# Cross heads turned on TensorE instead of through transfers, and the residual on ScalarE and GpSimd, in a one-layer hybrid decoder step

## The chip, the cores and the metric

The kernel runs on one core of one Trainium2 chip. The metric is the device time of one execution in microseconds, as the median of several runs. PE is TensorE, DVE VectorE, ACT ScalarE, POOL GpSimd and SP SyncE, whose queue issues most DMA transfers here.

## What is computed

One inference step of a decoder layer, for 4096 new tokens of one sequence and for 8 x 8 tokens that continue cached sequences, all in float32 with a model width of 1024. The input is normalised and projected to 2816 columns. These feed three groups of heads: a gated short convolution (256 columns), sliding-window attention with window 128 (8 query heads, 2 key/value heads of width 64, one learned sink each), and cross attention with 4 heads into 256 memory tokens. The gated outputs, 1024 columns, go through an output projection, a normalisation, and are added to the input.

```python
h = _rmsnorm(x, g_pre)
z = h @ w_in
cb, cc, ch, cg, q, k, v, ag, mq, mg = _split_cols(z)
...
o_b = _window_prompt(q, k, v, sink_g)
out_b = jax.nn.silu(ag) * o_b
o_c = _mem_attend(mq.reshape(n, t, MEM_HEADS, HEAD_DIM), mem_k, mem_v)
out_c = jax.nn.silu(mg) * o_c
y = jnp.concatenate([out_a, out_b, out_c], axis=-1) @ w_out
return x + _rmsnorm(y, g_post), new_conv, new_k, new_v
```

## The kernel before

The program has two stages. The first, the input projection, runs the three phases of `input_projection` and stores queries, keys, values and gates in DRAM; in its third phase it also computes the memory's keys and values and the attention of groups 0 and 1, and begins group 2 (`third_jobs`, `first_chunk`). The second stage is the attention and output projection of 32 blocks of 128 rows. This text calls one pass of its loop a round.

A *group* is the attention of one 128-row block: its scores on PE (`bands` into `ws`, `crosses` into `xs`), two softmaxes, and the products with the values (`values`, into `pv`). The stage is pipelined over groups: in round i, `values_and_scores` emits the scores of group i+3 and the values of group i+1, while `Block.run` projects block i. A block's projection is two halves of 512 output columns, `y` with p = 0 and p = 1, each of 24 matmuls (8 slices, and 3 products of high and low parts). `events_of` says at which half and slice of the block the other work is emitted.

The value product needs the probabilities transposed, with keys on the partitions. For groups 0 and 1 PE transposes them (`band_transposes`, `cross_transposes`). From group 2 on, `moved` does it: a VectorE instruction transposes every 32x32 square in place, then SP issues 16 transfers inside SBUF, each of 32 partitions by 256 columns (32 KB), that bring the squares to their partitions. `turn_band` does so for the window heads (tile `sm`, result `wt`), `turn_cross` for the cross heads (tile `xp`, result `xt`): 32 transfers a round. `masks` then has GpSimd cut the window out of `wt` with four selects (copies in `wd`). The cross heads' probabilities are scaled by GpSimd (`cross_weights`) before they are turned.

A block ends in two parts that are kept for the next round's `scores` (`tails`): `scale` squares the second half on ScalarE and takes the reciprocal root (its power on GpSimd, tile `yst`), and `store` adds the scaled result `yn` to the input rows `xr` with one VectorE instruction and stores `xr`. There are two `xr` buffers and one `yn`. The load of a later block's `xr` waits on SP for the store from the same buffer.

A planner orders the instructions of each engine. VectorE's, from round 1 to 30, are held to the order in which the program emits them, as are the transposes of the squares, the masks, and the split of a block's input into `mh` and `ml`. In `tiled`, a run of attention matmuls is held to program order after its first; the output projection's matmuls are placed by the planner. `work` hands out tiles of 1024 columns from a pool of three.

In PSUM, `ws` has banks b0 to b3, `xs` b4 and b5, the first half of `y` shares b0, and `pv` has two banks of which the second half of `y` uses one. The few decode tokens are handled by `sample_mem` and `sample_window`, whose steps are spread over rounds 26 to 30; their loads (`sq`, `svm`, `skc`, `svc`) go through SP too.

Of the kernel before, what the change touches and what calls it, by code (L numbers as in the profile page):

```python
# [8 lines left out]
F32 = mybir.dt.float32  # L9
# [3 lines left out]
ALU = mybir.AluOpType  # L13
AX = mybir.AxisListType

P = 128
D = 1024
KT = D // P
# [33 lines left out]
def hybrid_layer(ctx: ExitStack, tc: tile.TileContext, a: dict):  # L52
# [1059 lines left out]
    class Group:  # L1112
# [3 lines left out]
            self.chunk, self.i, self.b = chunk, i, 2 * chunk.c + i  # L1116
            self.pt, self.pv, self.xpt, self.cross_sums = {}, {}, {}, {}

        def open_scores(self, n):
            b = self.b  # L1120
            if n == 0:
                t = wp.tile([P, D], F32, tag="sm", name=f"sm{b}", bufs=1) if b % 2 and b > 1 else work(f"sm{b}")
                self.sm = t.rearrange("p (h k j) -> p h k j" if b < 2 else "p (k h j) -> p h k j", h=8, k=4)
                self.flat_sm = t
            if n == 3:
                t = wp.tile([P, D], F32, tag="p", name=f"xp{b}", bufs=1) if b % 2 and b > 1 else work(f"xp{b}")
                self.p = t.rearrange("p (h a k j) -> p h a k j" if b < 2 else "p (k h a j) -> p h a k j", h=4, a=2, k=4)
                self.flat_p = t

        def early_scores(self, n):  # L1130
            self.open_scores(n)
# [12 lines left out]
        def scores(self):  # L1144
            self.open_scores(0)
            self.open_scores(3)
# [75 lines left out]
        def early_transposes(self, n):  # L1222
            if n == 0:
                pt = work(f"wpt{self.b}").rearrange("p (u n) -> p u n", u=2)
                pv = work(f"wpv{self.b}").rearrange("p (u n) -> p u n", u=2) if self.b else None
                for u in range(2):
                    self.pt[u], self.pv[u] = pt[:, u], pv[:, u] if self.b else None
            if n == 2:
                xpt = work(f"xpt{self.b}").rearrange("p (u n) -> p u n", u=2)
                for u in range(2):  # L1230
                    self.xpt[u] = xpt[:, u]
            if n < 2:
                self.band_transposes(n, psum(0, f"wt{self.b}_{n}"))
            else:
                self.cross_transposes(n - 2, psum(0, f"xt{self.b}_{n}"))

        def moved(self, squares, name):

            tc.keep_in_program_order(V.transpose(squares, squares))
            to = wp.tile([P, 4, 256], F32, tag=name, name=f"{name}{self.b}")  # L1240
            src = squares.rearrange("p (k n) -> p k n", k=4)
            for g in range(4):
                for k in range(4):
                    DMA.dma_start(to[32 * k : 32 * k + 32, g], src[32 * g : 32 * g + 32, k])
            return to

        def turn_band(self):
            self.w = self.moved(self.flat_sm, "wt").rearrange("p g (h i) -> p g h i", h=8)
# [26 lines left out]
        def cross_transposes(self, u, t):  # L1275
            t3 = t.rearrange("p (k n) -> p k n", k=2)
            for kt in range(2):
                for j in range(2):
                    TE.transpose(t3[:, kt, j * P : (j + 1) * P], self.p[:, 2 * u + j, kt].rearrange("p k j -> p (k j)"), ident)
            (S.copy if u else V.tensor_copy)(self.xpt[u], t)  # L1280

        def cross_values(self, o):
            c = self.chunk
            for j in range(2):
                x = (lambda hh, kt: self.xpt[hh][:, CT * kt + P * j : CT * kt + P * j + P]) if self.b < 2 else lambda hh, kt: self.x[:, :, 2 * hh + j, kt]
# [145 lines left out]
    def sample_window():  # L1431
# [22 lines left out]
        both = work("ssm")[:, : 4 * 192].rearrange("p (a n) -> p a n", a=4)  # L1454
# [30 lines left out]
        pt, ptn = work("swpt").rearrange("p (a n) -> p a n", a=2)[:, 0], work("swptn")[:64, :512]  # L1485
# [21 lines left out]
    class Block:  # L1507
# [28 lines left out]
        def run(self, last, events):  # L1536
# [6 lines left out]
            for p, (c0, c1) in enumerate(parts):  # L1543
# [6 lines left out]
                for k in range(KT):  # L1550
                    for fn in events.get((min(p, 1), k), ()) if p < 2 else ():
                        fn()
                    for l, r in ((0, 0), (1, 0), (0, 1)) if m == P else ((0, 0), (0, 1)):
                        TE.matmul(acc, self.hl[l][:, k], wo[k][c0 // 512][:, r, c0 % 512 : c0 % 512 + c1 - c0], start=j == 0, stop=j == passes * KT - 1)  # L1554
                        j += 1
                if m < P:
                    S.copy(yn[:m, c0:c1], acc[m : 2 * m])
# [19 lines left out]
                    V.tensor_tensor(yn[:m, 768:D], acc[:m], gpost[:m, 768:D], op=ALU.mult)  # L1577

            def store():
                for cs in (slice(0, 512), slice(512, D)) if last else (slice(0, D),):  # L1580
                    V.scalar_tensor_tensor(self.xr[:m, cs], yn[:m, cs], st[:m, 3:4], self.xr[:m, cs], op0=ALU.mult, op1=ALU.add)  # L1581
                    DMA.dma_start(dst[:, cs], self.xr[:m, cs])
# [23 lines left out]
    def events_of(i):  # L1606

        ev = {}

        def at(p, k, fn, *args):  # L1610
            ev.setdefault((p, k), []).append(lambda: fn(*args))

        at(0, 0 if i else 3, values_and_scores, i)
        if i + 2 < len(blocks):
            at(0, 0, blocks[i + 2].load)
        if i % 2 == 0:
            at(0, 1 if i else 4, chunk_load, i // 2 + 3)
# [135 lines left out]
```

## Time and profile before

| | |
|---|---|
| median of 3 runs | 1812.81 us (1812.52 to 1813.56) |
| the profiled execution | 1814.48 us, span 1812.8 us |
| PE busy | 1537.6 us (85%) |
| weight loads | 1380.1 us (76%) |
| VectorE busy | 1197.3 us (66%) |
| ScalarE busy | 732.0 us (40%) |
| GpSimd busy | 344.2 us (19%) |
| mean granted PE clock | 0.926 |
| SP's queue | 262.47 MB in 194501 packets |
| transfers inside SBUF | 480 `wt<-sm`, 480 `xt<-xp`, 32 KB each |

The profile is one execution. Rows of a group give the line, the engine, the operation, output and inputs by the program's names, the shapes and the count, then the busy time, the mean duration of one, and the idle time of the engine just before with what ended it. Line 62 stands for all VectorE instructions of rounds 1 to 30, and line 1044 for all attention matmuls, so these groups are told apart by their tiles. Rows of a timeline give start, length and a merged run of like instructions. Rows of stretches give start and end, the length, the busy times, the granted PE clock as a share of full speed, the share of the 16 DMA engines' time that was busy, and GB/s.

### The profile page before, as it was taken

To read this page: it belongs to the slowest core of one execution; us is meant where nothing else is said; L and a number is where in the kernel's file an instruction comes from. 1 tells how busy PE (TensorE), PEld (TensorE's weight loads), DVE (VectorE), ACT (ScalarE), POOL (GpSimd) and SP (SyncE) were. 2 spreads that over 40 slices of the span, in tenths; PEclk is the share of its full clock that TensorE was granted. 3 is DMA by queue.
4 is the path that set the end of the run, shared out by engine and by line. 5 is a ranking of instruction groups with operands and counts; after the bars stand their busy time and mean duration, and the time that the engine had idled before them with its cause. 6 is when DMAs were issued, how large, how long until landed. Compare 5 with 4: busy or idle time off the path is not lost. (4 is left out here: it accounts for less than half of the span.)

```text
span 1812.8 us, 31491 instructions
## 1 busy us (share of the span) xinstructions
PE 1537.6 (85%) x11471; PEld 1380.1 (76%) x11471; DVE 1197.3 (66%) x1920; ACT 732.0 (40%) x1844; POOL 344.2 (19%) x522
## 2 busy tenths in 40 slices
PE   9999999999999999999995776678667766777548
PEld 9999999999999999999994555456555555555336
DVE  7788888998877797677684654455546545654414
ACT  6766565642222244454362333333333333333212
POOL 0223332230000000001002322233123223322200
PEclk9999999999999999999997898888888888988679
DMA  9989998776432379677877455543554554343342
GB/s 259 215 230 268 269 237 297 245 211 233 165 107 107 121 258 306 222 238 231 247 286 204 131 158 156 154 113 121 150 156 133 155 156 138 111 136 116 121 157 82
DMA packets 236175, 335.29 MB, mean 185 GB/s; under 512 B 62453, under 2 KB 164853, under 8 KB 235989
## 3 DMA queue, kind: packets, MB, share of 16 engines
q1 hardware_dynamic: 194501, 262.47, 46.9%
q0 software_dynamic: 40800, 69.76, 14.8%
q8 instruction: 91, 1.49, 0.4%
q10 hardware_dynamic: 720, 1.05, 0.2%
q14 instruction: 63, 0.52, 0.1%
HBM read 192.54 MB, written 110.15 MB: 167 GB/s over the span
## 5 line engine op out<-in xcount | busy, mean ns | idle before, releaser
L1554 PE MATMUL y<-wo,mh 128*128 128x512 f32 (+1 forms) x1040 | 340.2, 400 | 41.3 <-DVE sm L62 13.1
L1554 PEld LDWEIGHTS y<-wo,mh 128*128 128x128 f32 x1040 | 198.4, 192 | 103.1 <-issue 33.5
L377 DVE TENSOR_TENSOR z<-c,z 128x520 f32<-128x520 f32 (+1 forms) x308 | 195.0, 646 | 88.8 <-PE c L370 88.0
L1554 PE MATMUL y<-wo,ml 128*128 128x512 f32 (+1 forms) x520 | 204.8, 394 | 0.0
L1044 PE MATMUL pv<-xt,mv 128*64 128x128 f32 x480 | 54.4, 398 | 176.6 <-DMA xt<-xp 108.8
L1044 PEld LDWEIGHTS pv<-xt,mv 128*64 128x64 f32 x480 | 43.9, 207 | 188.2 <-issue 181.8
L1212 ACT ACTIVATE xp<-xs,xnm 128x256 f32<-128x256 f32 x128 | 58.9, 473 | 260.8 <-issue 127.7
L1220 POOL TENSOR_SCALAR xp<-xp,xrd 128x256 f32<-128x256 f32 x128 | 62.4, 502 | 490.5 <-DVE xrd L62 404.0
L1195 ACT ACTIVATE sm<-sm,wnm 128x128 f32<-128x128 f32 x256 | 99.1, 389 | 116.9 <-DVE wnm L62 113.8
L62 DVE TENSOR_TENSOR mix<-mix,pv 128x256 f32<-128x256 f32 (+1 forms) x32 | 16.3, 551 | 159.0 <-PE pv L1044 153.8
L1554 PEld LDWEIGHTS y<-wo,ml 128*128 128x128 f32 x520 | 100.2, 193 | 20.5 <-issue 2.0
L62 DVE TENSOR_TENSOR place<-place,pv 128x256 f32<-128x256 f32 (+1 forms) x28 | 14.3, 551 | 134.3 <-PE pv L1044 134.3
L1178 ACT COPY sm<-ws 128x256 f32<-128x256 f32 x128 | 41.2, 376 | 68.1 <-PE ws L1044 43.2
L1562 ACT ACTIVATE y<-y 128x512 f32<-128x512 f32 (+1 forms) x66 | 38.4, 582 | 72.4 <-DVE yn L62 63.8
L1258 POOL TENSOR_SCALAR_AFFINE_SELECT wd<-wt 128x512 f32<-128x512 f32 (+1 forms) x60 | 60.8, 1013 | 32.0 <-DMA wt<-sm 16.5
L1044 PEld LDWEIGHTS ws<-kst,q 64*128 64x128 f32 x768 | 48.9, 190 | 11.6 <-issue 5.6
L62 DVE SCALAR_TENSOR_TENSOR xr<-yn,yst,xr 128x1024 f32<-128x1024 f32 x30 | 42.8, 1427 | 21.1 <-POOL yst L1575 21.0
L1044 PE MATMUL ws<-kst,q 64*128 64x256 f32 x768 | 56.5, 293 | 0.0
L1044 PE MATMUL pv<-wt,vh 128*64 128x256 f32 x240 | 53.0, 583 | 0.0
L745 POOL MEMSET negs<- 128x1 f32 x1 | 0.1, 98 | 264.4 <-PE c L370 264.4
L283 ACT ACTIVATE nat<-nat 104x1024 f32<-104x1024 f32 x40 | 42.2, 1056 | 15.7 <-DMA nat<-in_x_p 15.7
L1195 ACT ACTIVATION_READ_ACCUMULATOR sm<-sm,wnm 128x1 f32 x256 | 48.1, 188 | 0.0
(979 smaller groups left out, 4971.0 us busy)
## 6 DMA issues: line engine op xcount, KB each, us to landing
q<-qd POOLq DMA_DIRECT2D x32, 768.0 KB, 9.1
xr<-in_x_p SPq DMA_DIRECT2D x32, 512.0 KB
nat<-in_x_p SPq DMA_DIRECT2D x39, 416.0 KB
o_yp<-xr SPq DMA_DIRECT2D x31, 512.0 KB
wt<-sm SPq DMA_DIRECT2D x480, 32.0 KB
xt<-xp SPq DMA_DIRECT2D x480, 32.0 KB
md<-th POOLq DMA_DIRECT2D x48, 260.0 KB, 7.4
qd<-zh SPq DMA_DIRECT2D x48, 260.0 KB
```

The lines of the kernel that those rows point to most:

```text
L62: return (lambda *args, **kw: tc.keep_in_program_order(fn(*args, **kw))) if self.on else fn
L283: S.activation(t[:RG], t[:RG], AF.Square, accum_out=r[:RG, i : i + 1])
L377: add = lambda dst, other: V.tensor_tensor(dst, c, other, op=ALU.add)
L745: G.memset(third["negs"], NEG)
L1044: ins = TE.matmul(o, w, x, **kw)
L1178: S.copy(to, squares(s3[:, :, P : 2 * P]))
L1195: S.activation(sm[:, h], sm[:, h], AF.Exp, bias=nm[:, h : h + 1], scale=SCALE, accum_out=den[:, h : h + 1])
L1212: S.activation(p[:, i], s[:, i].rearrange("p (a k j) -> p a k j", a=2, k=4), AF.Exp, bias=nm[:, i : i + 1], scale=SCALE, accum_out=den[:, ...
L1220: G.tensor_scalar(p[:, i], p[:, i], rd[:, i : i + 1], 0.5, op0=ALU.mult, op1=ALU.mult)
L1258: G.affine_select(out, src, pattern=[[32 * sign, 2], [0, 8], [sign, 32]], compare_op=op, fill=0.0, base=base * sign, channel_multiplier=-s ...
L1554: TE.matmul(acc, self.hl[l][:, k], wo[k][c0 // 512][:, r, c0 % 512 : c0 % 512 + c1 - c0], start=j == 0, stop=j == passes * KT - 1)
L1562: square = lambda acc=acc, p=p, c0=c0, c1=c1, end=end: S.activation((psum(2, "sq") if end else acc)[:m, : c1 - c0], acc[:m], AF.Square, sc ...
```

## The change

The cross heads of all groups are now transposed on PE. `turn_cross` calls `cross_transposes` twice, on banks b1 and b2, which makes eight 128x128 transposes and two ScalarE copies into tiles `xpt`. `moved` is gone; `turn_band` keeps its in-place square transpose and its 16 transfers. The transposes come at the start of the block's second half for group i+2, and the masks of group i+2 right behind them instead of in the first half; the first slice of each half, and each slice at which something is emitted, starts with a matmul that is held in program order.

`store` scales `yn` on ScalarE and adds it to `xr` on GpSimd, in place of the one VectorE instruction (but for the last block and the decode block).

The pool `work` has one 1024-column tile instead of three, and one tile of 2048 columns, `pair`; a group's window and cross probabilities lie in one 2048-column tile, in `pair` for even groups (and for groups 0 and 1) and in a tile of `wp` for odd ones. The decode window's tiles are cut from `pair` too.

```diff
-        third["work"] = right.enter_context(tc.tile_pool(name="work", bufs=3, side="right"))
+        third["work"] = right.enter_context(tc.tile_pool(name="work", bufs=1, side="right"))
...
+    def pair(name):
+        return third["work"].tile([P, 2 * D], F32, tag="uu", name=name)
+
+    def in_order_here(ins):
+        if ps is not None:
+            tc.keep_in_program_order(ins)
...
-        def open_scores(self, n):
+        def open_scores(self):
             b = self.b
+            t = wp.tile([P, 2 * D], F32, tag="s", name=f"s{b}", bufs=1) if b % 2 and b > 1 else pair(f"s{b}")
+            self.flat_sm, self.flat_p = t[:, :D], t[:, D:]
...
-        def moved(self, squares, name):
-            tc.keep_in_program_order(V.transpose(squares, squares))
-            to = wp.tile([P, 4, 256], F32, tag=name, name=f"{name}{self.b}")
-            src = squares.rearrange("p (k n) -> p k n", k=4)
+        def turn_band(self):
+            tc.keep_in_program_order(V.transpose(self.flat_sm, self.flat_sm))
+            to = wp.tile([P, 4, 256], F32, tag="w", name=f"w{self.b}")
+            squares = self.flat_sm.rearrange("p (k n) -> p k n", k=4)
             for g in range(4):
                 for k in range(4):
-                    DMA.dma_start(to[32 * k : 32 * k + 32, g], src[32 * g : 32 * g + 32, k])
-            return to
+                    DMA.dma_start(to[32 * k : 32 * k + 32, g], squares[32 * g : 32 * g + 32, k])
+            self.w = to.rearrange("p g (h i) -> p g h i", h=8)
...
         def turn_cross(self):
-            self.x = self.moved(self.flat_p, "xt").rearrange("p g (h a i) -> p g h a i", h=4, a=2)
+            for u in range(2):
+                self.xpt[u] = wp.tile([P, 512], F32, tag="xpt", name=f"xpt{self.b}_{u}")
+                self.cross_transposes(u, psum(1 + u, f"xt{self.b}_{u}"))
...
-                    TE.transpose(t3[:, kt, j * P : (j + 1) * P], self.p[:, 2 * u + j, kt].rearrange("p k j -> p (k j)"), ident)
-            (S.copy if u else V.tensor_copy)(self.xpt[u], t)
+                    in_order_here(TE.transpose(t3[:, kt, j * P : (j + 1) * P], self.p[:, 2 * u + j, kt].rearrange("p k j -> p (k j)"), ident))
+            S.copy(self.xpt[u], t)
...
+                    ordered = b > 0 and (j == 0 or p < 2 and (min(p, 1), k) in events)
...
+                        if ordered:
+                            tc.keep_in_program_order(ins)
+                        ordered = False
...
             def store():
+                if not last and b != 32:
+                    tc.keep_in_program_order(S.mul(yn, yn, st[:, 3:4]))
+                    G.tensor_tensor(self.xr, yn, self.xr, op=ALU.add)
+                    DMA.dma_start(dst, self.xr)
+                    return
...
-        if i == 0:
-            at(0, 4, turn, 1, 2)
-        at(0, 4, turn, 2, i + 2)
+        at(1, 0 if i else 2, turn, 1, i + 2)
+        at(1, 1, turn, 2, i + 2)
...
         at(1, 2, turn, 0, i + 3)
-        at(1, 2, turn, 1, i + 3)
```

More of the change, by code (lines that the diff above doesn't have):

```diff
@@ L1117, in __init__, with early_scores @@
             self.pt, self.pv, self.xpt, self.cross_sums = {}, {}, {}, {}
-        def open_scores(self, n):
+        def open_scores(self):
             b = self.b
-            if n == 0:
[L1122 to L1131, printed above, removed]
+            t = wp.tile([P, 2 * D], F32, tag="s", name=f"s{b}", bufs=1) if b % 2 and b > 1 else pair(f"s{b}")
+            self.flat_sm, self.flat_p = t[:, :D], t[:, D:]
+            self.sm = self.flat_sm.rearrange("p (h k j) -> p h k j" if b < 2 else "p (k h j) -> p h k j", h=8, k=4)
+            self.p = self.flat_p.rearrange("p (h a k j) -> p h a k j", h=4, a=2, k=4)
+        def early_scores(self, n):
+            if n == 0:
+                self.open_scores()
             if n < 2:
@@ L1144, in scores @@
         def scores(self):
-            self.open_scores(0)
-            self.open_scores(3)
+            self.open_scores()
             bands = [psum(n, f"ws{self.b}_{n}").rearrange("p (h k) -> p h k", h=2) for n in range(4)]
@@ L1224, in early_transposes @@
                 pt = work(f"wpt{self.b}").rearrange("p (u n) -> p u n", u=2)
-                pv = work(f"wpv{self.b}").rearrange("p (u n) -> p u n", u=2) if self.b else None
+                pv = self.flat_sm.rearrange("p (u n) -> p u n", u=2) if self.b else None
                 for u in range(2):
@@ L1235, in early_transposes @@
                 self.cross_transposes(n - 2, psum(0, f"xt{self.b}_{n}"))
-        def moved(self, squares, name):
-            tc.keep_in_program_order(V.transpose(squares, squares))
-            to = wp.tile([P, 4, 256], F32, tag=name, name=f"{name}{self.b}")
-            src = squares.rearrange("p (k n) -> p k n", k=4)
+        def turn_band(self):
+            tc.keep_in_program_order(V.transpose(self.flat_sm, self.flat_sm))
+            to = wp.tile([P, 4, 256], F32, tag="w", name=f"w{self.b}")
+            squares = self.flat_sm.rearrange("p (k n) -> p k n", k=4)
             for g in range(4):
                 for k in range(4):
-                    DMA.dma_start(to[32 * k : 32 * k + 32, g], src[32 * g : 32 * g + 32, k])
-            return to
-        def turn_band(self):
-            self.w = self.moved(self.flat_sm, "wt").rearrange("p g (h i) -> p g h i", h=8)
+                    DMA.dma_start(to[32 * k : 32 * k + 32, g], squares[32 * g : 32 * g + 32, k])
+            self.w = to.rearrange("p g (h i) -> p g h i", h=8)
         def turn_cross(self):
-            self.x = self.moved(self.flat_p, "xt").rearrange("p g (h a i) -> p g h a i", h=4, a=2)
+            for u in range(2):
+                self.xpt[u] = wp.tile([P, 512], F32, tag="xpt", name=f"xpt{self.b}_{u}")
+                self.cross_transposes(u, psum(1 + u, f"xt{self.b}_{u}"))
         def masks(self):
@@ L1284, in cross_values @@
             for j in range(2):
-                x = (lambda hh, kt: self.xpt[hh][:, CT * kt + P * j : CT * kt + P * j + P]) if self.b < 2 else lambda hh, kt: self.x[:, :, 2 * hh + j, kt]
+                x = lambda hh, kt: self.xpt[hh][:, CT * kt + P * j : CT * kt + P * j + P]
                 both_values(o[:, j * P : j * P + P], *([(third["mv"][:, kt, j * P : (j + 1) * P], x(hh, kt)) for kt in range(2)] for hh in range(2)))
@@ L1453, in sample_window @@
         transpose_to(svn, [(zs[:, 5, :], 64)], 1, "svnt")
-        both = work("ssm")[:, : 4 * 192].rearrange("p (a n) -> p a n", a=4)
+        ssm = pair("ssm")
+        both = ssm[:, : 4 * 192].rearrange("p (a n) -> p a n", a=4)
         sms = [both[:, 2 * half : 2 * half + 2] for half in range(2)]
@@ L1484, in sample_window @@
         yield
-        pt, ptn = work("swpt").rearrange("p (a n) -> p a n", a=2)[:, 0], work("swptn")[:64, :512]
+        pt, ptn = ssm[:, D : D + 512], ssm[:64, D + 512 : 2 * D]
         transpose_to(pt, [(sm[i][:, 0:P], P) for i in range(4)], 1, "swt0")
@@ L1552, in run @@
                         fn()
+                    ordered = b > 0 and (j == 0 or p < 2 and (min(p, 1), k) in events)
                     for l, r in ((0, 0), (1, 0), (0, 1)) if m == P else ((0, 0), (0, 1)):
-                        TE.matmul(acc, self.hl[l][:, k], wo[k][c0 // 512][:, r, c0 % 512 : c0 % 512 + c1 - c0], start=j == 0, stop=j == passes * KT - 1)
+                        ins = TE.matmul(acc, self.hl[l][:, k], wo[k][c0 // 512][:, r, c0 % 512 : c0 % 512 + c1 - c0], start=j == 0, stop=j == passes * KT - 1)
+                        if ordered:
+                            tc.keep_in_program_order(ins)
+                        ordered = False
                         j += 1
```

## The prediction

> **What bounds the kernel now.** I read the busy times by stage first, then the waits of TensorE and of SyncE's DMA queue in the stage that has room, then that queue in order of time.
>
> ```profile
> span 1812.8 us, 31491 instructions
> ```
>
> ```profile
> 0.00:960.00 960.00, 949.23 (x7812) 934.87 (x7812) 770.23 (x1107) 463.01 (x813) 129.27 (x194) 1.00 0.75 227
> ...
> 992.90:1664.00 671.10, 476.82 (x3016) 363.23 (x3017) 360.26 (x676) 227.23 (x884) 187.17 (x284) 0.86 0.49 139
> ```
>
> After each stretch and its length stand the busy times of PE, weight load, DVE, ACT and POOL, the granted clock, the DMA share and GB/s. The input projection (to 960) keeps PE busy for 949 of 960 us at full clock, so nothing can be won there. The attention stage from the first `pv` (992.9) to the 27th (1664.0) is 26 rounds of one 128-row block: 671.1 / 26 = 25.81 us a round. No engine is busy for three quarters of it, and the PE clock is 0.86.
>
> ```profile
> L1554 PE MATMUL y<-wo,mh 128*128 128x512 f32 x832 | 275.5, 403 | 29.2 <-DVE sm L62 12.0 <-DVE mix L62 8.8 <-DVE place L62 8.2
> L1044 PE MATMUL pv<-xt,mv 128*64 128x128 f32 x416 | 49.1, 410 | 169.2 <-DMA xt<-xp 101.4 <-DMA o_yp<-xr 67.8
> ```
>
> ```profile
> SPq L1516 <- DMA o_yp<-xr: 70.3, 13, 6.4
> ```
>
> These are two PE groups of this window (busy time, mean ns, idle time before them) and a wait of SP. PE idles 169.2 / 26 = 6.5 us a round before the cross heads' value product, for DMAs of SP's queue, and 29.2 / 26 = 1.1 us before the output product. SP itself waits 70.3 / 26 = 2.7 us a round for a block's store, before it reloads that buffer.
>
> ```profile
> 1314.55 10.38 SPq L1244 DMA_DIRECT2D xt<-xp  x16
> 1325.02 0.53 SPq L1582 DMA_DIRECT2D o_yp<-xr  x1
> 1325.65 0.38 SPq L1090 DMA_DIRECT2D place<-md  x1
> 1331.32 0.34 SPq L1516 DMA_DIRECT2D xr<-in_x_p  x1
> 1331.75 0.38 SPq L1110 DMA_DIRECT2D vh<-vn  x1
> 1332.31 10.39 SPq L1244 DMA_DIRECT2D wt<-sm  x16
> ...
> 1662.66 0.53 SPq L1582 DMA_DIRECT2D o_yp<-xr  x1
> 1663.29 0.38 SPq L1110 DMA_DIRECT2D vh<-vn  x1
> 1663.84 1.95 SPq L1244 DMA_DIRECT2D wt<-sm  x3
> 1665.88 0.53 SPq L1516 DMA_DIRECT2D xr<-in_x_p  x1
> ```
>
> This is SP's queue: start, time, what it issues. It has no gap but the one after the store: two sets of sixteen 32 KB moves at 10.4 us are 20.8, store, loads and `vh` 1.5, the wait 2.7, together 25.0 of the round's 25.81. **Issuing on SP is the bound**; PE waits for the last of the 32 moves.
>
> **The change, part by part.**
>
> *Sixteen moves off SP.* How long one set takes depends on what else the DMA engines do (length, clock, DMA share, GB/s of three sets):
>
> ```profile
> 964.70:981.20 16.50, 0.81 1.04 273
> ...
> 1314.50:1325.00 10.50, 1.00 0.57 130
> ...
> 1641.30:1652.40 11.10, 0.90 0.40 131
> ```
>
> Up to a share of 0.57 it is 10.4 to 11.1 us; with the engines full it is 16.5. A shorter round raises the mean share from 0.49, the half of the moves that goes lowers it; I take 11.1. From a store to the reload behind it go 6.3 us (1325.02 to 1331.32) when a 1 MB gate load is in flight, which is every second round, else at most 3.2 (1662.66 to 1665.88). With 0.8 or 0.4 for the other issues that is 11.1 + 6.3 + 0.8 = 18.2 and 11.1 + 3.2 + 0.4 = 14.7, a mean of 16.5 us a round. SP falls below the new PE sum, by little.
>
> *Eight transposes onto PE, and the stall off it.* The round on a warm PE comes from these rows:
>
> ```profile
> 1150.74:1156.37 5.63, 5.63 (x24) 1.00 0.21 55
> ```
>
> ```profile
> 1156.37 1.69 PE L1044 MATMUL ws<-kst,q 64*128 64x256 f32 x24
> 1157.90 0.88 PE L1044 MATMUL xs<-mk,q 64*128 64x256 f32 x12
> ```
>
> ```profile
> 820.44 0.60 PE L1279 MATMUL xt<-ident,xp 128*128 128x128 f32 x4
> 820.79 0.36 PE L370 MATMUL c<-hi_4T,w_0S 128*128 128x260 f32 x1
> ```
>
> ```profile
> 1302.70:1307.00 4.30, 3.89 (x32) 0.68 0.67 197
> ...
> 1704.70:1707.30 2.60, 2.60 (x35) 0.97 0.21 55
> ```
>
> A half of `y` takes 5.63 (24 matmuls, clock 1.00), two are 11.3. Scores go from 1156.37 to 1158.78, 2.4. Four transposes hold PE from 820.44 to 820.79, so two sets are 0.7. The last two rows are the 32 value products: 2.6 us on a warm PE, 3.9 at clock 0.68 after a wait. Sum 11.3 + 2.4 + 2.6 + 0.7 = 17.0 us. Today's round agrees: 16.3 without transposes, 7.6 of waits, 1.9 left for what runs at a low clock after each wait; if the wait goes, that goes too. I take 1.1 us of small waits as left, the size of today's second wait group though their places move: **18.1 us a round**. Bounds: 17.0 with none, 20 with what the rivals add.
>
> *Order on PE.* Today `y` half 0, values, `y` half 1, scores; then scores, values, `y` half 0, transposes, `y` half 1. Values follow at once on the scores. They share PSUM banks with the last block's `y` half 1, which a DVE and an ACT pass of 512 columns must first drain; at 0.6 each (by the ACT copy below) that is 1.2 us under 2.4 of scores. `y` half 1, which today waits for the gate product (`mix` and `place` in the row above), gets 6.3 us of cover. The masks move into the second half. In DVE's order the band's transpose stands behind `y` half 0 and its multiply: 2.4 + 2.6 + 5.6 + 0.6 + 1.2 = 12.2 us from the scores. Then 11.1 of moves, at most 3.2 to land (as the store) and 3.6 of masks make 30, against two rounds and the scores, 38.6. These 8 us are the cover; without it PE stands still, since nothing is queued between scores and values.
>
> *The other engines.*
>
> ```profile
> L62 DVE SCALAR_TENSOR_TENSOR xr<-yn,yst,xr 128x1024 f32<-128x1024 f32 x26 | 37.7, 1449 | 19.8 <-POOL yst L1575 19.6
> ...
> L62 DVE STREAM_TRANSPOSE xp<-xp 128x1024 f32<-128x1024 f32 x26 | 32.3, 1244 | 4.4 <-POOL xp L1220 4.4
> ```
>
> ```profile
> L1280 ACT COPY xpt<-xt x2: 586/586/587, 824.4 to 876.4; 128x512 f32<-128x512 f32 x2
> ```
>
> ```profile
> L1195 ACT ACTIVATE sm<-sm,wnm 128x128 f32<-128x128 f32 x208 | 80.5, 388 | 106.1 <-DVE wnm L62 106.1
> ...
> L1530 ACT CAST mh<-mix 128x1024 fp32r<-128x1024 f32 x14 | 14.6, 1040 | 0.0
> ```
>
> ```profile
> L1220 POOL TENSOR_SCALAR xp<-xp,xrd 128x256 f32<-128x256 f32 x104 | 47.8, 475 | 407.0 <-DVE xrd L62 389.1 <-DMA wt<-sm 17.9
> L1258 POOL TENSOR_SCALAR_AFFINE_SELECT wt<-wt 128x512 f32<-128x512 f32 x52 | 37.1, 737 | 1.7
> L1258 POOL TENSOR_SCALAR_AFFINE_SELECT wd<-wt 64x512 f32<-64x512 f32 x26 | 30.9, 1188 | 1.8
> L1258 POOL TENSOR_SCALAR_AFFINE_SELECT wd<-wt 128x512 f32<-128x512 f32 x26 | 24.2, 929 | 24.3 <-DMA wt<-sm 12.5 <-DMA xt<-xp 6.7 <-PE xs L1044 3.0
> ```
>
> ```profile
> L459 POOL TENSOR_TENSOR us<-z,z 128x64 f32<-128x64 f32 x2 | 6.6, 3298 | 34.9 <-DVE z L377 34.9
> ...
> L476 POOL TENSOR_TENSOR cacc<-cacc,z 128x64 f32<-128x64 f32 x4 | 1.6, 393 | 0.3
> ```
>
> DVE loses a transpose (1.24) and the residual (1.45): 360.26 / 26 = 13.9 becomes 11.2 us a round. ACT gains two copies at 0.59 and a 1024-wide scale at 1.04: 8.7 becomes 10.9. The scale waits for the power on POOL and stands ahead of the eight exponentials, which today wait 106.1 / 26 = 4.1 us a round for DVE's maximum; that covers it. Without the cover it costs 1 us. POOL's 128x1024 add has no row. From below, four 256-wide multiplies, 1.9 us; from above, sixteen 64-wide adds at 0.39, 6.3. I take 1.9, the row nearest in shape. POOL goes from 7.2 to 9.1 (at most 13.5), still under 17. Behind the add stand the masks (0.93 + 1.19 + 2 x 0.74 = 3.6) and the cross scaling, before which POOL idles 407.0 / 26 = 15.7 us a round. The add frees `yn` after drain 1.2, power, scale 1.0 and add 1.9, an estimated 5 to 7 us into the round, and the next block wants it when `y` half 0 ends, after 10.6. The Trainium skill (GPSIMD Engine Reference, 3.1 Elementwise) gives 4497 ns for an add of 2048 fp32 columns on this engine, an estimate of 2.2 us here, inside those bounds; no run so far shows it.
>
> *Fewer, larger buffers.* Even and odd groups have one 2048-wide tile each. Group g+2 writes it two rounds after g; its last readers, moves and transposes, end one round after g's scores. That round is the cover, so nothing. In the projection PE's instructions keep their order, and its 949 busy us hide the rest.
>
> *The end.*
>
> ```profile
> PE sms L1398 <- DMA sq<-in_cmk: 33.1, 4, 14.1
> ```
>
> After 1664.0 PE waits 33.1 us for loads that SP issues behind 32 moves. They now come ahead of, or behind, sixteen. Bounds 0 and 33.1; I take 20, since the value loads still stand behind moves. At the start (960 to 992.9) the values no longer wait for a second set of moves, but come ahead of a `y` half: nothing.
>
> **Sum.** 26 x (25.81 - 18.1) = 200, and 20: 220 us off the span of 1812.8 is 1593. The profiled run took 1814.48, its span and 1.7 around it; the median of the runs, 1812.81, is 1.7 below that run, so 1593 stands for the median too.
>
> **The rivals.**
>
> *SP stays the bound.* For it: 16.5 against 17.0 is close, and a faster round crowds the DMA engines. With moves half way to full engines, 13.8, the rounds are 20.9 and 17.4, a mean of 19.2: 172 + 20 off, 1621. Against: the `xt` set of 1314.55 kept 10.4 at a share of 0.57.
>
> *DVE and POOL get in each other's way.* If DVE stood still through add, masks and cross scaling (1.9 + 3.6 + 1.9 = 7.4), it would need 11.2 + 7.4 = 18.6, with handoffs 20: 151 + 20 off, 1642. Against: the select on `wt` takes 737 ns, on `wd` 929 in the same shape, so neighbours cost POOL tenths, not multiples. The Trainium skill (SBUF — State Buffer, Who interferes with whom) says that a DVE instruction with two SBUF inputs and a GpSimd instruction that reads SBUF lock each other out. By that rule only some of DVE's instructions are hit (not the maximum, nor the gate with its PSUM input), so it would make less than this case.
>
> *Another chain holds the round.* 67.8 of the 169.2 us are put down to the store, so the named DMA may not be what PE waited for. If scores, softmax, gate and split held the round at 24, it would be 47 off, 1766. Against: SP's own sum of 25.0 leaves no room for another.
>
> *No waits left.* 17.0 a round and 33 at the end: 229 + 33 off, 1551.
>
> *Slower.* POOL's add at the rate of the costly 64-wide product, 3298 ns times sixteen, takes 52.8 us: POOL then needs 60 a round, 26 x 34 more, 2700. It decides once the add takes over 25.8 - 7.2 = 18.6 us. Against: the other 64-wide row is 393 ns.
>
> **How the numbers follow.** Forecast 0.50, SP 0.22, DVE and POOL 0.10, no waits 0.07, another chain 0.07, slower 0.04. The range goes from somewhat below the no-wait case to somewhat above the DVE case: 1538 to 1660. 0.2% (3.6 us) is what a measurement here tells from no change. Faster 0.95, within it 0.01, slower 0.04.
>
> **What would show it.** `pv` with almost no idle before it, a PE clock near 1.0 from 1000 us on, 16 moves a round with a gap on SP before them, rounds of 17 to 19 us, POOL's add at 1.9 to 2.5 us. It is wrong if `pv` still waits several us a round: then the releaser names the chain that I missed (masks, or the store behind the add).

## The result, and the profile after

The changed kernel takes 1547.67 us (median of 4 runs, 1544.48 to 1549.3) against 1812.69 us: a ratio of 0.8535, with a 95% interval of 0.8519 to 0.8551. The prediction of 1593 was 45 us too long; the time came out next to the rival that I had called "no waits left" (1551).

Three stretches of the changed kernel (span 1547.6 us), cut at its first `pv` (988.5) and its 27th (1438.9):

```profile
960.00:988.50 28.50, 13.48 (x79) 10.81 (x77) 12.40 (x26) 10.31 (x39) 7.17 (x12) 0.80 1.07 274
988.50:1438.90 450.40, 443.92 (x3224) 352.49 (x3224) 356.53 (x624) 275.33 (x963) 242.80 (x312) 0.99 0.66 178
1438.90:1547.60 108.70, 94.56 (x611) 71.38 (x607) 50.65 (x109) 41.47 (x122) 31.68 (x40) 0.95 0.44 141
```

The 26 rounds took 450.4 us, 17.32 each, where they took 671.1. PE's busy time in them fell by 33 us (476.82 to 443.92, at a clock of 0.99 in place of 0.86) although it executes 208 more matmuls (8 a round); its idle time fell by 188 us (194.3 to 6.5). With 4.4 us at the start (32.9 to 28.5) and 40.1 at the end (148.8 to 108.7) the three stretches make 265.2 us, the whole difference of the spans.

What PE still waits for from 960 us on (us in all, times, longest):

```profile
PE y L1558 <- ACT y L1569: 11.5, 2, 9.9
PE pv L1052 <- ACT y L1569: 11.2, 7, 5.1
PE smo L1416 <- DMA svm<-in_cmv: 6.3, 1, 6.3
```

The `pv` waits on moves (169.2 us) and the `y` waits on VectorE (29.2) are gone. What is left at `pv` is 11.2 us in all, of which 5.1 lie ahead of the first `pv`, before the 26 rounds. One round in which PE never stops, its `y` products left out:

```profile
1022.38 1.69 PE L1052 MATMUL ws<-kst,q 64*128 64x256 f32 x24
...
1024.72 1.09 PE L1052 MATMUL pv<-xpt,mv 128*64 128x128 f32 x16
...
1032.80 1.04 PE L1281 MATMUL xt<-ident,s 128*128 128x128 f32 x8
1039.22 1.69 PE L1052 MATMUL ws<-kst,q 64*128 64x256 f32 x24
```

From scores to scores it is 16.84 us (1022.38 to 1039.22): that is PE's own round, and from the second of the 26 to the ninth each takes 16.84 to 16.87. The first takes 19.3, and from the tenth on most are longer; PE first waits for `pv` again at 1194.7, and this is the longest of these waits:

```profile
1370.08 1.09 PE L1052 MATMUL pv<-xpt,mv 128*64 128x128 f32 x16 [2.03 <-ACT y L1569]
```

The mean of 17.32 has 0.48 us more than PE's own round, and SyncE's queue, later in the stage, shows why:

```profile
1299.50 10.69 SPq L1247 DMA_DIRECT2D w<-s  x16
1310.29 0.53 SPq L1098 DMA_DIRECT2D mix<-md  x1
1310.92 0.52 SPq L1590 DMA_DIRECT2D o_yp<-xr  x1
1311.53 0.38 SPq L1118 DMA_DIRECT2D vh<-vn  x1
1317.83 0.33 SPq L1519 DMA_DIRECT2D xr<-in_x_p  x1
1318.27 12.77 SPq L1247 DMA_DIRECT2D w<-s  x16
1331.14 0.53 SPq L1118 DMA_DIRECT2D vh<-vn  x1
1331.77 0.38 SPq L1590 DMA_DIRECT2D o_yp<-xr  x1
1335.02 0.33 SPq L1519 DMA_DIRECT2D xr<-in_x_p  x1
1335.45 9.92 SPq L1247 DMA_DIRECT2D w<-s  x15
```

One set of sixteen moves a round is left. The two gaps stand between a block's store and the load behind it, and there is no other: from store to load it is 6.9 us (1310.92 to 1317.83) and 3.3 us (1331.77 to 1335.02). From set to set it is 18.8 and 17.2 us here; over the twenty sets from 1075.46 to 1425.11 the mean is 17.5. So SP still has the longer round, by some 0.6 us. The early rounds at 16.85 fit that: a set that comes later from round to round costs PE nothing until its cover is used up.

The work that the change put on ScalarE and GpSimd, and two small VectorE groups that come back below:

```profile
L1589 POOL TENSOR_TENSOR xr<-yn,xr 128x1024 f32<-128x1024 f32 x26 | 62.5, 2402 | 16.7 <-ACT yn L1588 16.4
...
L1588 ACT ACTIVATE yn<-yn,yst 128x1024 f32<-128x1024 f32 x26 | 29.9, 1150 | 42.0 <-POOL yst L1582 42.0
```

```profile
L62 DVE SCALAR_TENSOR_TENSOR wnm<-wmx,nsink 128x8 f32<-128x8 f32 x26 | 34.3, 1319 | 0.9
L62 DVE TENSOR_SCALAR xnm<-xmx 128x2 f32<-128x2 f32 x52 | 32.7, 629 | 1.8
```

### The profile page after: what moved, and what is told of

It is laid out like the page before. It is cut to its first block, busy times and chain, and to the rows that moved or that the text cites. A ratio compares the mean times of both kernels' runs of the same rounds, so it can differ in the third digit from the quotient of the medians.

```text
span 1547.6 us, 31556 instructions
## 1 busy us (share of the span) xinstructions
PE 1501.4 (97%) x11711; PEld 1370.1 (89%) x11711; DVE 1185.1 (77%) x1857; ACT 790.4 (51%) x1937; POOL 408.3 (26%) x553
## 4 chain that ended last, share of the span: by engine, by line
PE 62%; DMA 14%; DVE 7%; issue 5%; SPq 5%; ACT 3%; POOL 3%; ACTq 0%; POOLq 0%; DVEq 0%
PE c L370 43%; PE y L1558 12%; SPq L1247 4%; DMA w<-s 4%; DMA o_yp<-xr 3%; PE pv L1052 3%; PE ws L1052 2%; DMA nat<-in_x_p 1%; PE xt L1281 1%; ACT s L1199 1%; DMA x_0B<-in_xt 1%; PE mem_acc L786 1%; PE xs L1052 1%; DVE s L62 1%; DMA xr<-in_x_p 1%
## 5 line engine op out<-in xcount | busy, mean ns | idle before, releaser
L1558 PE MATMUL y<-wo,mh 128*128 128x512 f32 (+1 forms) x1040 | 338.6, 396 | 11.5 <-ACT y L1569 11.5
L1199 ACT ACTIVATE s<-s,wnm 128x128 f32<-128x128 f32 x256 | 99.0, 388 | 41.3 <-DVE wnm L62 38.1
L1182 ACT COPY s<-ws 128x256 f32<-128x256 f32 x128 | 41.3, 379 | 112.4 <-PE ws L1052 75.2
L1260 POOL TENSOR_SCALAR_AFFINE_SELECT wd<-w 128x512 f32<-128x512 f32 (+1 forms) x60 | 51.5, 858 | 151.5 <-DMA w<-s 139.8
L1224 POOL TENSOR_SCALAR s<-s,xrd 128x256 f32<-128x256 f32 x128 | 61.6, 497 | 111.6 <-DVE xnm L1214 60.0
L1589 POOL TENSOR_TENSOR xr<-yn,xr 128x1024 f32<-128x1024 f32 x31 | 74.4, 2400 | 23.7 <-ACT yn L1588 23.4
L62 DVE TENSOR_TENSOR yn<-y,gpost 128x512 f32<-128x512 f32 x60 | 41.4, 689 | 37.1 <-PE y L1558 35.3
L62 DVE COPY_PREDICATED s<-wmask,ws 128x256 f32<-128x256 uint8 x112 | 43.6, 442 | 30.2 <-ACT s L1182 17.0
L1216 ACT ACTIVATE s<-xs,xnm 128x256 f32<-128x256 f32 x128 | 58.3, 463 | 4.3 <-DVE xnm L1214 3.2
L1052 PEld LDWEIGHTS ws<-kst,q 64*128 64x128 f32 x768 | 47.8, 185 | 11.2 <-issue 9.9
L283 ACT ACTIVATE nat<-nat 104x1024 f32<-104x1024 f32 x40 | 42.2, 1055 | 11.4 <-DMA nat<-in_x_p 11.4
L1199 ACT ACTIVATION_READ_ACCUMULATOR s<-s,wnm 128x1 f32 x256 | 48.0, 187 | 0.0
L1260 POOL TENSOR_SCALAR_AFFINE_SELECT w<-w 128x512 f32<-128x512 f32 x60 | 46.4, 796 | 2.1
```

The costliest lines, as they stand in the source:

```text
L62: return (lambda *args, **kw: tc.keep_in_program_order(fn(*args, **kw))) if self.on else fn
L283: S.activation(t[:RG], t[:RG], AF.Square, accum_out=r[:RG, i : i + 1])
L1052: ins = TE.matmul(o, w, x, **kw)
L1199: S.activation(sm[:, h], sm[:, h], AF.Exp, bias=nm[:, h : h + 1], scale=SCALE, accum_out=den[:, h : h + 1])
L1216: S.activation(p[:, i], s[:, i].rearrange("p (a k j) -> p a k j", a=2, k=4), AF.Exp, bias=nm[:, i : i + 1], scale=SCALE, accum_out=den[:, ...
L1224: G.tensor_scalar(p[:, i], p[:, i], rd[:, i : i + 1], 0.5, op0=ALU.mult, op1=ALU.mult)
```

## The experiments

Theory: SP's issuing of 32 moves a round set the time before, and with sixteen gone PE and SP are nearly level. Rivals: it was the bytes that the moves carry, not their issue; the residual's move to other engines has a part in the gain; so has the later place of the masks.

### The residual alone

The kernel after with the old residual on VectorE:

```diff
             def store():
-                if not last and b != 32:
-                    tc.keep_in_program_order(S.mul(yn, yn, st[:, 3:4]))
-                    G.tensor_tensor(self.xr, yn, self.xr, op=ALU.add)
-                    DMA.dma_start(dst, self.xr)
-                    return
```

> The changed kernel with the residual back on VectorE in one instruction. If PE's own 17 us set the round, VectorE has room for the 1.45 us more (some 11 to 14 busy us a round) and the time stays within 1 percent of 1548, 1535 to 1560. Rival: the move of the residual to ScalarE and GpSimd is what shortened the round; then 30 to 60 us come back, 1580 to 1610.

It took 1546.25 us, ratio 0.8498 (0.8468 to 0.8528). And the kernel before with these five lines added and nothing else:

> The kernel before with only the new residual. If SP's 32 issues a round are the bound, VectorE's 1.45 us less buys nothing: 1805 to 1820, or up to 25 us more where the later store holds SP's reload longer (1 us a round). Rival: VectorE's order held the round before too; then 1.4 us a round are gained, 1775.

It took 1819.94 us against 1816.83, ratio 1.0013 (0.999 to 1.0035). Its PE still waits as before, 161.8 us for these two where the kernel before has 169.2:

```profile
PE pv L1044 <- DMA xt<-xp: 133.1, 22, 8.4
PE pv L1044 <- DMA o_yp<-xr: 28.7, 4, 9.3
```

So the residual's move takes nothing off, neither alone nor beside the rest. The first of these two kernels shows why. The same stretch of it, and the two small VectorE groups in it:

```profile
988.50:1438.90 450.40, 440.09 (x3185) 349.54 (x3186) 326.53 (x649) 248.57 (x936) 180.90 (x285) 0.99 0.66 176
```

```profile
L62 DVE SCALAR_TENSOR_TENSOR xr<-yn,yst,xr 128x1024 f32<-128x1024 f32 x26 | 33.3, 1279 | 27.2 <-POOL yst L1582 27.2
...
L62 DVE TENSOR_SCALAR xnm<-xmx 128x2 f32<-128x2 f32 x52 | 8.8, 169 | 1.8
...
L62 DVE SCALAR_TENSOR_TENSOR wnm<-wmx,nsink 128x8 f32<-128x8 f32 x26 | 4.3, 167 | 0.9
```

VectorE has the residual here (33.3 us) and is yet busy for 30.0 us less than in the kernel after (326.53 against 356.53). Its other work therefore grew by 63.3 us in the kernel after, and 53.9 of that is in two groups that are tiny: `wnm` went from 4.3 to 34.3 us and `xnm` from 8.8 to 32.7. GpSimd's 26 adds take 62.5 us. The kernel after has them side by side; first GpSimd's timeline, then VectorE's:

```profile
1303.70 2.40 POOL L1589 TENSOR_TENSOR xr<-yn,xr 128x1024 f32<-128x1024 f32 x1 [1.26 <-ACT yn L1588]
...
1318.05 2.41 POOL L1589 TENSOR_TENSOR xr<-yn,xr 128x1024 f32<-128x1024 f32 x1
```

```profile
1303.91 2.22 DVE L62 TENSOR_SCALAR xnm<-xmx 128x2 f32<-128x2 f32 x1
...
1317.91 2.58 DVE L62 SCALAR_TENSOR_TENSOR wnm<-wmx,nsink 128x8 f32<-128x8 f32 x1
```

A VectorE instruction of 8 columns lasts from 1317.91 to 1320.49, to the end of the add (1320.46), and one of 2 columns from 1303.91 to 1306.13, where the add beside it ends at 1306.10. In the kernel before, the five added lines raise `wnm` as well, from 187 to 1157 ns in the mean; `xnm` stays at 169 there. The add takes 1.28 us off VectorE and holds it for about 2.4. It costs no time only because VectorE, at 356.53 / 26 = 13.7 us a round, has 3.6 to spare.

### The sixteen moves back on SP, and their bytes without the issues

The kernel after with each of the sixteen moves issued a second time into a tile that nothing reads:

```diff
+            again = wp.tile([P, 4, 256], F32, tag="again", name=f"again{self.b}", bufs=1)
+            for g in range(4):
+                for k in range(4):
+                    DMA.dma_start(again[32 * k : 32 * k + 32, g], squares[32 * g : 32 * g + 32, k])
```

> The changed kernel that issues each of the sixteen moves of a group a second time, into a tile that nobody reads. If issuing on SP is the bound of the kernel before, the queue needs 2 x 10.4 to 11.1 and 5 us a round again, 26 to 27, and the time is 1770 to 1830 although PE has its transposes. Rival: PE waited for the transposed cross heads, not for the queue; then nothing waits for the copies and it stays at 1548 to 1580.

One run: 1815.96 us, the time of the kernel before (1816.83 beside it), with a clock that is down again. A window of its stage, a wait of PE from 985 us on, and SP's queue:

```profile
985.00:1440.00 455.00, 322.10 (x2151) 252.67 (x2151) 235.68 (x413) 182.59 (x635) 162.30 (x200) 0.84 0.52 141
```

```profile
PE pv L1052 <- ACT y L1573: 190.9, 27, 15.1
```

```profile
1339.01 10.89 SPq L1247 DMA_DIRECT2D w<-s  x16
1349.95 10.09 SPq L1251 DMA_DIRECT2D again<-s  x16
```

The releaser named is "ACT y", though ScalarE's work is what it was and only SP's grew. A wait for several events carries the name of the one that came last in the records. The waits for "ACT y" at `pv` in the kernel after have to be read with the same care.

The same 512 KB by one DMA, in rows of 1 KB:

```diff
+            again = wp.tile([P, 4, 264], F32, tag="again", name=f"again{self.b}", bufs=1)
+            DMA.dma_start(again[:, :, :256], squares)
```

> The same 512 KB more a round, also in rows of 1 KB, but as one transfer. If the number of issues counts, SP has 0.5 us more a round and the time is 1548 to 1575. Rival: the bytes and packets on the DMA engines count (their share was 0.66, with these some 0.77); then it is nearer to the run with sixteen, over 1650.

One run: 1594.04 us, 46 over the kernel after, so outside what I gave it. PE waits for SP's work again, and SP's round is longer: 19.1 us from set to set in the mean (1082.45 to 1426.50), where the kernel after has 17.5.

```profile
PE pv L1052 <- ACT y L1571: 39.4, 13, 7.4
```

```profile
1340.33 0.66 SPq L1249 DMA_DIRECT2D again<-s  x1
...
1341.76 1.13 SPq L1592 DMA_DIRECT2D o_yp<-xr  x1
...
1349.46 0.33 SPq L1521 DMA_DIRECT2D xr<-in_x_p  x1
```

The sets themselves are no slower, 11.5 us in the mean against 11.4. The one issue takes about 0.8 us with the step behind it, and from the store to the load go 5.7 us in the mean (7.7 in the rows above) in place of 4.8.

Sixteen issues more cost 268 us (1815.96 - 1547.67), the same bytes in one issue 46. Most of the price of the moves, some 222 us, is their number. The 46 are not nothing, because SP has no slack in the kernel after: 1.6 us a round more counts at once, about half of it the one issue and half the longer way from store to load beside the extra bytes. The one transfer goes from a partition to itself, where the moves cross partitions, and each of the two kernels ran once, so this bounds the bytes' share and does not measure it exactly.

The kernel with the moves twice keeps every other part of the change: the residual, the place of the masks, the matmuls held in order, the fewer buffers. None of them gains anything there. Whether the order and the buffers matter once SP has room, no run here shows.

### The transposes twice

```diff
-                self.cross_transposes(u, psum(1 + u, f"xt{self.b}_{u}"))
+                bank = psum(1 + u, f"xt{self.b}_{u}")
+                for kt in range(2):
+                    for j in range(2):
+                        in_order_here(TE.transpose(bank.rearrange("p (k n) -> p k n", k=2)[:, kt, j * P : (j + 1) * P], self.p[:, 2 * u + j, kt].rearrange("p k j -> p (k j)"), ident))
+                self.cross_transposes(u, bank)
```

> The changed kernel that makes each of the eight transposes of a group a second time into the same bank. If PE sets the round, 0.7 us more a round cost 30 x 0.7 = 21 us and the time is 1560 to 1572. Rival: SP's queue sets it (a pair of rounds on SP took 35.2 us); then PE has 0.4 us to spare a round and it is under 1558.

It took 1552.47 us, ratio 0.8546 (0.8521 to 0.8572): 5 more, not 12 to 24, so the time of the rival (under 1558). Its 26 rounds, cut at its own first and 27th `pv`:

```profile
984.70:1447.60 462.90, 462.90 (x3432) 375.46 (x3428) 353.11 (x624) 276.20 (x961) 256.40 (x312) 0.99 0.64 177
```

PE has no idle time at all in these rounds (462.90 of 462.90). They take 17.80 us, which is 0.9 to 1.0 for eight transposes over PE's own round (16.84, and 16.91 as a mean in a run below). Yet the rounds grew by 12.5 us in all, not by 23, since 17.32 already held some 0.4 us that SP costs PE, and that now lies under PE's work; the start and the end are 3.8 and 6.1 us shorter (24.7 and 102.6). So PE and SP are level within a microsecond, and a little more work on PE is half hidden by SP.

### Taking the wait out of SP's round

If SP's wait for its own store holds the kernel after at 17.32, taking it away must give PE's 16.85. First, three buffers for `xr` in place of two:

```diff
-            self.xr = yp.tile([P, D], F32, tag="xr", name=f"xr{b}")
+            self.xr = yp.tile([P, D], F32, tag="xr", name=f"xr{b}", bufs=3)
```

> The changed kernel with three buffers for the residual's rows instead of two, so that SP's reload does not wait for the last store. If SP holds part of the changed kernel's rounds (17.3 us against 16.85 in its quickest), they fall to 16.9: 26 x 0.4 = 11 us, 1533 to 1542. Rival: PE alone sets them; then it is within 3 us of 1547.

It took 1553.34 us, ratio 0.8546 (0.8523 to 0.8568): no gain, and the wait was still there:

```profile
SPq L1519 <- DMA o_yp<-xr: 108.0, 25, 7.0
```

With a third buffer the planner moved each load forward, to stand again right behind the store that frees its buffer. The same kernel with the sample's memory values loaded from GpSimd's queue:

```diff
-            DMA.dma_start(vm[:, j], a["cmv"][j][:, bs])
+            G.dma_start(vm[:, j], a["cmv"][j][:, bs])
```

> The same with the decode step's value loads issued by GpSimd instead of behind sixteen moves on SP. If the 6.3 us that PE waits for them at the end go, it is 4 to 7 us below the run with three buffers alone. Rival: the wait moves to the next load or to the softmax; then there is no difference.

It took 1546.75 us, ratio 0.8511 (0.8491 to 0.853), 6.6 less than without; the `smo` wait of 6.3 us at the end was gone. Then three buffers with each load held a store later:

```diff
-            self.xr = yp.tile([P, D], F32, tag="xr", name=f"xr{b}")
-            DMA.dma_start(self.xr[:m], a["x_s"] if b == 32 else a["x_p"][b * P : (b + 1) * P, :])
+            self.xr = yp.tile([P, D], F32, tag="xr", name=f"xr{b}", bufs=3)
+            ins = DMA.dma_start(self.xr[:m], a["x_s"] if b == 32 else a["x_p"][b * P : (b + 1) * P, :])
+            if 2 < b < 31:
+                tc.keep_in_program_order(ins)
...
-        if i + 2 < len(blocks):
-            at(0, 0, blocks[i + 2].load)
+        if i > 0:
+            at(0, 0, blocks[i + 1].load)
+        if i == 30:
+            at(0, 0, blocks[32].load)
```

> The kernel after with three buffers for the residual's rows and each load placed a store later, so that on SyncE's queue the load behind the store of one block fills the buffer that was stored a round before. Theory (SyncE's wait of some 6 us in each pair of rounds keeps it level with TensorE): that wait is gone (it was 31 waits of 6.7 us behind o_yp), rounds fall from 17.32 to TensorE's own 16.85, 26 x 0.47 = 12 less: 1533 to 1542. Rival (TensorE's round holds the 0.47 for other reasons, such as the copies between transposes): the wait goes and the time stays, 1545 to 1555.

It took 1527.64 us, ratio 0.8419 (0.8405 to 0.8434), 20 less than the changed kernel, below the range that I gave it, and the best median here. (The 6.7 us in the expectation is the longest of the 31 waits; together they are 130.1.) SP's queue and its longest wait, then two stretches cut at the first and 27th `pv`:

```profile
1316.60 0.38 SPq L1592 DMA_DIRECT2D o_yp<-xr  x1
1317.03 0.42 SPq L1519 DMA_DIRECT2D xr<-in_x_p  x1
1322.18 11.04 SPq L1247 DMA_DIRECT2D w<-s  x16
```

```profile
SPq L1247 <- DVE s L62: 106.0, 27, 5.9
```

```profile
988.50:1428.10 439.60, 439.58 (x3226) 352.95 (x3226) 357.30 (x625) 276.36 (x963) 257.17 (x313) 1.00 0.66 187
1428.10:1528.80 100.70, 91.87 (x609) 70.31 (x607) 53.28 (x109) 41.14 (x122) 30.51 (x38) 0.99 0.40 130
```

The load goes out 0.4 us behind the store, and SP's gap now stands before the next set, where it waits for VectorE's transpose: SP has room. Rounds are 439.6 / 26 = 16.91 us, and PE is busy for 439.58 of 439.60. Of the 18.8 us between the spans 10.8 are from the rounds and 8.0 from the end, where the `smo` wait fell from 6.3 to 0.9 as well. I had counted only the rounds.

Both edits together:

> The same, with the sample's memory values loaded from GpSimd's queue. In the kernel with three buffers whose wait remained this took 6.6 us off the end. Theory: it takes 5 to 7 off here too, 1527 to 1537, the best of all. Rival: 1538 to 1550, as with that change alone.

It took 1533.97 us, ratio 0.8451 (0.8429 to 0.8474): nothing more (the single runs go from 1526.01 to 1538.12), since the wait that the second edit takes away had gone with the first.

### The place of the masks

```diff
-        at(1, 1, turn, 2, i + 2)
+        at(0, 4, turn, 2, i + 2)
```

> The kernel after with the masks' turn put back to the earlier place in the block's products, and nothing else. Theory (the masks have some 8 us of slack in a round): within 1% of 1548, 1533 to 1563. Rival (the later place is part of the gain, since the masks wait for moves that are not there yet and hold GpSimd's queue ahead of the residual's add and the rest): over 1570.

It took 1551.91 us, ratio 0.8562 (0.8543 to 0.858): within 0.3% of the kernel after. The place of the masks is no part of the gain.

### SP's load put on another queue in the kernel before

Two ways to relieve SP there without PE. First the cross heads' sixteen moves issued by ScalarE:

```diff
-        def moved(self, squares, name):
+        def moved(self, squares, name, queue=DMA):
...
-                    DMA.dma_start(to[32 * k : 32 * k + 32, g], src[32 * g : 32 * g + 32, k])
+                    queue.dma_start(to[32 * k : 32 * k + 32, g], src[32 * g : 32 * g + 32, k])
...
-            self.x = self.moved(self.flat_p, "xt").rearrange("p g (h a i) -> p g h a i", h=4, a=2)
+            self.x = self.moved(self.flat_p, "xt", S).rearrange("p g (h a i) -> p g h a i", h=4, a=2)
```

> The kernel before with the cross heads' sixteen moves issued by ScalarE instead of SP: same transfers, same bytes, two issuers. If issuing is the bound, SP falls to some 16 us a round and ScalarE rises to 8.7 + 10 = 19, with the moves ahead of the next split; the round is 19 to 22 and the time 1640 to 1715. Rival: the transfers themselves (their bytes, their landing) are the bound; then it stays over 1780.

One run: 1892.28 us, slower than before, and in the range of the rival (over 1780). ScalarE's timeline, a set of SP's beside its second set, and waits of ScalarE and PE:

```profile
1313.38 14.40 ACTq L1244 DMA_DIRECT2D xt<-xp  x16
1327.82 1.04 ACT L1530 CAST mh<-place 128x1024 fp32r<-128x1024 f32 x1 [16.01 <-DMA xt<-xp]
...
1344.36 10.17 ACTq L1244 DMA_DIRECT2D xt<-xp  x16
```

```profile
1343.31 10.23 SPq L1244 DMA_DIRECT2D wt<-sm  x16
```

```profile
ACT mh L1530 <- DMA xt<-xp: 364.2, 24, 27.0
```

```profile
PE y L1554 <- DVE sm L62: 269.6, 23, 15.3
```

The issues themselves do go side by side: sixteen on each queue in 10.2 us. Only in every second round are the sets longer, 14.2 to 16.7 us on ScalarE (14.02 on SP beside the 14.40). SP has room now, and waits 133.5 us for VectorE. So the rival's time came, but not by its cause: the split of the next block (`mh`), the scores' copies and the exponentials stand behind the sixteen on ScalarE, and PE waits before the output product `y`, which needs that split (the name `DVE sm` in its row is of the kind seen above; that the split is the cause is read from the order on ScalarE). ScalarE idles enough over a round as a whole for sixteen issues; the theory left out, or priced too low, what stands behind them in its order.

Then only the loads of `xr` issued by GpSimd, so that SP doesn't wait for its store:

```diff
-            DMA.dma_start(self.xr[:m], a["x_s"] if b == 32 else a["x_p"][b * P : (b + 1) * P, :])
+            G.dma_start(self.xr[:m], a["x_s"] if b == 32 else a["x_p"][b * P : (b + 1) * P, :])
```

> The kernel before with the loads of the residual's rows issued from GpSimd's queue, so that SyncE no longer stands behind its own store of a block before it loads into that buffer. Theory (in the kernel before, SyncE's queue sets the round, and its 2.7 us of waiting for the store count in full): 26 rounds lose 2.5 to 3.5 us each, 1720 to 1750. Rival 1 (the moves of both kinds wait for the chain of squares and masks, not for SyncE): 1800 to 1815. Rival 2 (the wait goes to GpSimd's queue, stands ahead of the masks there, and comes back by them): 1815 or more.

One run: 1989.2 us, so the second rival. GpSimd's timeline, its waits and PE's:

```profile
1416.77 0.56 POOL L1516 DMA_DIRECT2D xr<-in_x_p  x1 [19.99 <-DMA o_yp<-xr]
```

```profile
POOL xr L1516 <- DMA o_yp<-xr: 306.0, 20, 21.7
```

```profile
PE pv L1044 <- POOL wt L1258: 248.8, 11, 24.8
```

GpSimd stands still for 20 us at the load, with two groups' masks behind it (eight selects from 1417.33 on), and PE stands still for the masks. This is the kernel before, so it does not measure the cover of 8 us that the prediction gave the masks after the change.

## Why the prediction was right, and where it was off

**The bound.** "Issuing on SP is the bound" holds. Putting sixteen issues back gives the old time to within 1 us (one run), their bytes in one issue give 46 of the 268 us, and the residual and the masks' place give nothing. That neither attempt to take load off SP in the kernel before gained does not speak against it: the one put sixteen issues and the other a wait ahead of other work on an engine that computes.

**PE's round.** The sum of 17.0 us was right: 16.84 in the row above, 16.91 as a mean once SP has room. Its terms are off by little: eight transposes cost 0.9 where I took 0.7, and scores and values of that round 4.8 (1022.38 to 1027.2) where I took 5.0. The step that failed is "I take 1.1 us of small waits as left": the `y` waits on VectorE went from 29.2 us to none, since the second half of `y` has scores, values and the first half ahead of it, the cover that the same text named. Instead some 0.4 a round came from SP: that much goes when its wait goes (17.32 to 16.91). That is 26 x (18.1 - 17.32) = 20 of the 45 us.

**"SP falls below the new PE sum, by little."** This step failed the other way. I forecast 18.2 and 14.7 us for rounds with and without a slow store, 16.5 in the mean. From 1075.46 to 1425.11 they are 18.7 and 16.3, a mean of 17.5 against PE's own 16.9. The sets took 11.4 and not 11.1, from store to load the 4.8 that I took, and the other issues of a round 1.2 instead of 0.6; that last term is most of the miss. So the rival "SP stays the bound" was right in kind and far too dear: its 19.2 a round are 2.3 above PE's own, and 0.4 came. Its price rested on sets of 13.8; they took 10.2 to 13.2 at a DMA share of 0.66.

**The order on PE.** The terms behind the 12.2 us of the band's transpose add up to 12.4; nothing hangs on the difference.

**The end and the start.** "I take 20" was the second miss: the end gave 40.1, above the upper bound of 33.1 too. That bound held the `sms` wait alone. PE's idle time there fell from 53.3 us (148.80 - 95.47) to 14.1 (108.70 - 94.56): besides `sms`, 7.5 us at `pv` and 9.5 of the decode steps' waits for VectorE went, and 6.3 us at `smo` came. The start gave 4.4 where I took none; no run takes it apart. With the rounds' 20.3 and the end's 20.1 beyond forecast these make 44.8, the miss of 45.

**"No waits left".** That the time lies 3 us from this rival (1551) is in part luck. Its rounds of 17.0 would have given 229 us, and the 26 rounds gave 220.7; its end of 33 gave 40.1 and its start of nothing 4.4.

**The other engines.** GpSimd's add took 2.40 us where I took 1.9 from GpSimd's multiplies. The estimate of 2.2 from the Trainium skill (GPSIMD Engine Reference, 3.1 Elementwise) was nearer; the measured 2.40 decides. The scale on ScalarE took 1.15, not 1.04, and cost no time. VectorE's 11.2 us a round came out as 13.7.

**DVE and POOL in each other's way.** I gave this rival 7.4 us a round of standing still; the runs show 63.3 / 26 = 2.4, through the add alone, and 13.7 us is still under the bound, so it cost nothing. The rule that I weighed against it (the Trainium skill, SBUF — State Buffer, Who interferes with whom) is borne out where VectorE's instruction has two SBUF inputs, as `wnm` has (167 to 1319 ns in the mean). It says the same of a `tensor_scalar` in a fast mode that takes both port pairs, which fits `xnm` (169 to 629 ns), though these runs don't show the mode.

## What to carry to other kernels

Add up what one queue issues in a round, its waits included, before anything else: many small transfers cost by their number, and moving them to an engine with compute of its own blocks that engine in order, so the best place for the work may be an engine that needs no transfer at all. When a bound is removed, look at what is level with it next; here taking a load from right behind the store of its own buffer gave another 20 us, 10.8 of them in the rounds, and a third buffer helped only once the load no longer followed that store. Work given to GpSimd to relieve VectorE can hold VectorE for longer than it saves.

## What the hardware showed that I had not expected

A VectorE instruction of 2 or 8 columns can last as long as GpSimd's 1024-column add beside it: 2.22 and 2.58 us in place of 0.17. Its group's mean rises to 1319 ns, which in a profile looks like a costly instruction and is a wait.

Issuing a 32 KB move takes 0.65 us on SP (10.38 / 16, in the kernel before) and as little on ScalarE where its sets are quick (10.17 / 16 = 0.64), with SP issuing its own sixteen beside it in 10.23. But ScalarE does nothing else for that time.
